# One core: a small matrix product written with the matrix as stationary operand and two vectors as moving operand, without transposes

## The chip, the cores and the metric

The kernel runs on one core of a Trainium2 chip. The metric is the device time of one execution in microseconds (us). Times inside the program are counted from the start of the profiled span.

## What is computed

The reference is one layer of a diffusion backbone: an FFN, a mixer of a convolution branch and a recurrent branch, and a second FFN, on 512 latent tokens and 256 context tokens with 1024 channels. Every normalised input is multiplied by a scale and moved by a shift, which are linear in a conditioning vector: `c` for the latent tokens, `c_ctx` for the context. Cut to what matters here:

```python
m  = jnp.split((jax.nn.silu(c)     @ lp["w_mod"] + lp["b_mod"])[:, None, :],    N_MOD, axis=-1)
mc = jnp.split((jax.nn.silu(c_ctx) @ lp["w_mod"] + lp["b_mod"])[None, None, :], N_MOD, axis=-1)
x  = x  + 0.5 * m[2]  * swiglu(modulate(rmsnorm(x,  g_n1), m[0],  m[1]),  w_ffn1_up, w_ffn1_down)
xc = xc + 0.5 * mc[2] * swiglu(modulate(rmsnorm(xc, g_n1), mc[0], mc[1]), w_ffn1_up, w_ffn1_down)
```

`w_mod` is 1024 x 9216. The change concerns its first two of nine parts alone, the first shift (`m[0]`, `mc[0]`) and the first scale (`m[1]`, `mc[1]`), which the first FFN needs.

## The kernel before

Activations lie with channels on the 128 partitions: 1024 channels are 8 blocks k of 128. `mod_first(k)`, below called **block k**, computes shift and scale of channel block k for both vectors. It loads 1 MB of `w_mod` into two tiles named `raw` of 512 KB (the pool has four such tiles, `RB = 4`), multiplies on TensorE, and writes the columns k of the tiles `M[0]` (shift) and `M[1]` (scale). The trace shows each of these fp32 matmuls as two records (a weight load and a matmul record each, two times).

Around it the program starts up in these steps:

- x (2 MB) and xc (1 MB) are loaded, a position table is added to x (L609), squares are taken on ScalarE and summed on VectorE into `acc` (latent) and `accc` (context, both L279).
- Two matmuls with a matrix of ones (L283) sum `acc` and `accc` over the partitions. ScalarE and VectorE turn them into 1/rms, `rs` and `rsc` (L303 to L309). VectorE then writes `xr` = x times `rs` and xc times `rsc` (L617, L618), 16 instructions.
- `hook1` takes the channel blocks in turn: `scale_of` makes G (L263), ScalarE applies scale and shift to `xr` (L632), and VectorE and ScalarE form sums and differences of pairs of blocks (L356 to L359) and split each into a high and a low part (L146 on ScalarE, L147 on VectorE). These are the moving operands of the first FFN. The split parts have the names nh, nl, nhc, nlc and nbx.
- The weights of the first FFN (`up`) come through the same four `raw` tiles; their sums on VectorE are L393, L394, L397 and L398, and their split is `whi` (ScalarE) and `wlo` (VectorE). The first products run on TensorE in L425 to L427.
- From then on parts 2 to 8 of `w_mod` are computed on VectorE (L234, one load of 512 KB each) while the FFN runs.

Blocks 0 to 4 are called ahead of the sums of squares, blocks 5 to 7 inside `hook1`. The order in which each engine executes comes from a scheduler that plans the whole program; each engine and the DMA queue SP then work strictly in that order. A `raw` tile is loaded anew when its last reader is done.

Of the kernel before, what the change touches and what calls it, by code (L numbers as in the profile page):

```python
# [9 lines left out]
F32 = mybir.dt.float32  # L10
# [3 lines left out]
ALU = mybir.AluOpType  # L14

P = 128
D = 1024
KB = D // P
# [49 lines left out]
def block_kernel(ctx: ExitStack, tc: tile.TileContext, io):  # L68
# [6 lines left out]
    V, S, T, GP = nc.vector, nc.scalar, nc.tensor, nc.gpsimd  # L75
# [4 lines left out]
    def region(name, side=None):  # L80
        st = ExitStack()
        return st, st.enter_context(tc.tile_pool(name=name, bufs=1, side=side, reuse_waits="tile"))
# [24 lines left out]
    def psum_small():  # L107
        return PS["pool"].tile([P, 512], F32, name="psm", bufs=PS["singles"])
# [12 lines left out]
    def v_(name, a=0, b=None):  # L121
        o, s = VOFF[name]
        return vec[:, o + a:o + (s if b is None else b)]
# [9 lines left out]
    regA, A = region("regA", "right")  # L133
# [15 lines left out]
    def wload(src, n):  # L149
        raws = []  # L150
        for a in range(0, n, 1024):
            raw = wp.tile([P, 1024], F32, name="raw", bufs=RB)
            m = min(1024, n - a)
            last["load"] = nc.sync.dma_start(raw[:, :m], src[:, a:a + m])
            raws.append(raw)
        return raws
# [30 lines left out]
    def ps_both(ps):  # L187
# [2 lines left out]

    cs = const.tile([P, KB, 2], F32, name="cs")
    S.activation(cs.rearrange("p k j -> p (k j)"), v_("c"), AF.Silu)
    c32 = A.tile([P, KB, P], F32, name="c32", tag="cb1")
    V.memset(c32, 0.0)
    V.tensor_copy(c32.rearrange("p k (q r) -> p k q r", q=4)[:, :, :, 0:2],
                  cs[:, :, None, :].to_broadcast([P, KB, 4, 2]))

    def mod_first(k):
        ps = psum_small()
        raw = wload(io["wmod01"][k], 2048)  # L200
        last["mod"] = last["load"]
        for i in range(KB):
            T.matmul(ps[:, :256], c32[:, i, :], raw[i // 4][:, (i % 4) * 256:(i % 4 + 1) * 256],  # L203
                     start=(i == 0), stop=(i == KB - 1))
        tt = A.tile([P, 256], F32, name="tt", bufs=2)
        V.transpose(tt, ps[:, :256])
        tv = tt.rearrange("p (B q r) -> p B q r", B=2, q=4)
        for q in range(4):
            r = slice(32 * q, 32 * q + 32)
            for B in range(2):  # L210
                V.tensor_tensor(M[B][r, k, :], tv[r, B, q, 0:2],
                                v_("b_mod", B * KB + k, B * KB + k + 1)[r].to_broadcast([32, 2]), op=ALU.add)

    def mod_tile(i):
        return const.tile([P, KB, 2], F32, name=f"m{i}")
# [1 line left out]
    M, G = {}, {}  # L217
# [374 lines left out]
    er = pos[:, :32].rearrange("p (b r) -> p b r", b=4)  # L592
    ec = pos[:, 32:].rearrange("p (b r) -> p b r", b=4)
    mod_first(0)
    nc.sync.dma_start(pos, io["pos"])
    nc.sync.dma_start(x[:, :4], io["x"][:, :4])
    mod_first(1)
    nc.sync.dma_start(x[:, 4:], io["x"][:, 4:])
    nc.sync.dma_start(xc, io["xc"])
    for k in range(2, 5):  # L600
        mod_first(k)
# [60 lines left out]
    e, s_, s2, q, sp, rc = (la[:, i] for i in range(6))  # L662
# [30 lines left out]
    B = regB = None  # L693
# [405 lines left out]
```

## Time and profile before

| | us |
|---|---|
| median of 3 runs (1514.05 to 1519.76) | 1518.24 |
| the profiled execution, device time | 1522.92 |
| its span in the trace | 1521.1 |
| TensorE busy | 1436.9 (94%) |
| VectorE busy | 1267.5 (83%) |
| ScalarE busy | 730.1 (48%) |

The profiled execution is 4.7 us over the median; 1.8 us of its time lie outside the span. The shares are means over the whole program. The change acts in the first 5% of it, where TensorE and VectorE are loaded quite differently from the mean.

### The profile page before, as it was taken

Reading aid. Unit: us, or ns where it says so; the run is one execution under the profiler, and the core shown is the slowest. Engines: PE = TensorE matmul, PEld = TensorE weight load, DVE = VectorE, ACT = ScalarE, POOL = GpSimd, SP = SyncE. Lnnn points to the kernel's source line nnn. Section 1 sums busy time; section 2 is a strip of 40 time slices with the busy share of each in tenths; the row PEclk is TensorE's granted clock in tenths of the full one; section 3 lists DMA queues with packets and bytes.
Section 4 is the critical chain, followed back from the end, with each engine's and each line's share of the span. In section 5 each row is a group of like instructions: output and inputs, shape, how many; then the busy total and the mean of one; then the engine's idle time right before and its main releaser. Section 6 shows DMA issues by size and latency. Waiting matters only on the chain.

```text
span 1521.1 us, 20670 instructions
## 1 busy us (share of the span) xinstructions
PE 1436.9 (94%) x8094; PEld 1285.7 (85%) x8094; DVE 1267.5 (83%) x1957; ACT 730.1 (48%) x1011; POOL 22.2 (1%) x55
## 2 busy tenths in 40 slices
PE   6699999999999999899999989999996999999997
PEld 5498898989988997688778778778896989999897
DVE  5999999785768868899999999975589958678686
ACT  3742341422313345667887863236366525435252
POOL 0000000000000000000000040000000000000000
PEclk9799999999999999899999999999997999999999
DMA  7334445361425124112222212233251333323331
GB/s 279 128 125 159 147 148 163 111 194 56 145 94 186 62 83 160 62 63 90 70 64 97 77 54 85 77 131 139 97 181 56 91 118 98 97 98 98 111 98 56
DMA packets 49346, 169.02 MB, mean 111 GB/s; under 512 B 5600, under 2 KB 7904, under 8 KB 48608
## 3 DMA queue, kind: packets, MB, share of 16 engines
q1 hardware_dynamic: 49248, 167.70, 34.2%
q8 instruction: 63, 1.03, 0.3%
q14 instruction: 35, 0.29, 0.1%
HBM read 163.48 MB, written 4.19 MB: 110 GB/s over the span
## 4 chain that ended last, share of the span: by engine, by line
PE 58%; DVE 24%; DMA 7%; issue 7%; ACT 3%; POOLq 1%; DVEq 0%; ACTq 0%; POOL 0%; SPq 0%
PE psm L173 9%; PE psm L175 9%; PE psm L177 9%; PE psm L425 8%; PE psm L427 8%; PE psm L426 8%; DVE wlo L147 5%; DMA raw<-in_wmod 4%; DVE cv L742 3%; DMA raw<-in_down 2%; PE psm L203 2%; ACT whi L146 1%; DVE raw L234 1%; POOLq L1094 1%; DVE junk L234 1%
## 5 line engine op out<-in xcount | busy, mean ns | idle before, releaser
L146 ACT ACTIVATE whi<-raw 128x1024 fp32r<-128x1024 f32 (+2 forms) x230 | 233.1, 1014 | 352.0 <-PE psm L175 232.8
L147 DVE TENSOR_TENSOR wlo<-raw,whi 128x1024 fp32r<-128x1024 f32 (+2 forms) x230 | 267.4, 1163 | 37.7 <-ACT whi L146 37.4
L742 DVE SCALAR_TENSOR_TENSOR cv<-u,vec,cv 128x512 f32<-128x512 f32 x236 | 166.6, 743 | 1.0
L173 PE MATMUL psm<-H,whi 128*128 128x256 f32 (+1 forms) x496 | 152.0, 355 | 4.5 <-ACT H L146 4.1
L175 PE MATMUL psm<-H,whi 128*128 128x256 f32 (+1 forms) x496 | 151.9, 354 | 0.0
L177 PE MATMUL psm<-H,wlo 128*128 128x256 f32 (+1 forms) x496 | 151.0, 352 | 0.0
L173 PE MATMUL psm<-nh,whi 128*128 128x512 f32 x336 | 132.3, 396 | 4.2 <-ACT u L724 2.9
L177 PE MATMUL psm<-nh,wlo 128*128 128x512 f32 x336 | 132.0, 393 | 2.2 <-DVE wlo L147 2.1
L175 PE MATMUL psm<-nl,whi 128*128 128x512 f32 x336 | 132.1, 393 | 1.7 <-DVE nl L317 1.5
L425 PE MATMUL psm<-nbx,whi 128*128 128x384 f32 x286 | 98.3, 344 | 13.2 <-ACT nbx L146 7.8
L173 PEld LDWEIGHTS psm<-H,whi 128*128 128x128 f32 x496 | 92.9, 189 | 18.9 <-ACT H L146 5.6
L175 PEld LDWEIGHTS psm<-H,whi 128*128 128x128 f32 x496 | 93.5, 189 | 13.6 <-DVE H L147 0.5
L177 PEld LDWEIGHTS psm<-H,wlo 128*128 128x128 f32 x496 | 93.7, 189 | 13.0
L426 PE MATMUL psm<-nbx,whi 128*128 128x384 f32 x286 | 97.9, 342 | 0.8 <-DVE nbx L147 0.8
L427 PE MATMUL psm<-nbx,wlo 128*128 128x384 f32 x286 | 97.3, 342 | 0.4 <-DVE wlo L147 0.3
L425 PE MATMUL psm<-nb,whi 128*128 128x256 f32 x264 | 77.3, 293 | 10.4 <-ACT nb L146 9.2
L234 DVE SCALAR_TENSOR_TENSOR raw<-raw,cb 128x1024 f32<-128x1024 f32 x56 | 68.1, 1218 | 17.4 <-DMA raw<-in_wmod 17.2
L560 DVE SCALAR_TENSOR_TENSOR x<-psm,m,x 128x512 f32<-128x512 f32 x64 | 47.7, 745 | 39.6 <-PE psm L177 39.6
L146 ACT ACTIVATE whi<-s 128x1024 fp32r<-128x1024 f32 x44 | 46.7, 1062 | 70.0 <-PE psm L426 24.6
L426 PE MATMUL psm<-nl,whi 128*128 128x256 f32 (+1 forms) x264 | 79.9, 303 | 0.0
L173 PEld LDWEIGHTS psm<-nh,whi 128*128 128x128 f32 x336 | 63.3, 189 | 18.6 <-ACT u L724 3.2
L177 PEld LDWEIGHTS psm<-nh,wlo 128*128 128x128 f32 x336 | 63.4, 189 | 17.2 <-DVE wlo L147 4.0
(296 smaller groups left out, 3794.1 us busy)
## 6 DMA issues: line engine op xcount, KB each, us to landing
raw<-in_up SPq DMA_DIRECT2D x88, 512.0 KB, 3.8
raw<-in_wmod SPq DMA_DIRECT2D x72, 512.0 KB, 4.0
raw<-in_down SPq DMA_DIRECT2D x30, 512.0 KB, 4.0
raw<-in_down SPq DMA_DIRECT2D x24, 384.0 KB, 3.2
raw<-in_wvg SPq DMA_DIRECT2D x16, 512.0 KB, 3.7
raw<-in_wout SPq DMA_DIRECT2D x16, 512.0 KB, 3.9
raw<-in_wlx SPq DMA_DIRECT2D x10, 512.0 KB, 3.7
raw<-in_wlg SPq DMA_DIRECT2D x10, 512.0 KB, 3.7
```

Source lines behind the costliest of these rows:

```text
L146: S.activation(hi, src, AF.Copy)
L147: V.tensor_tensor(lo, src, f32(hi), op=ALU.subtract)
L173: T.matmul(p_, hi[:, wk, :], h, start=first, stop=False)
L175: T.matmul(p_, hi[:, wk, :], l, start=False, stop=False)
L177: T.matmul(p_, lo[:, wk, :], h, start=False, stop=last)
L203: T.matmul(ps[:, :256], c32[:, i, :], raw[i // 4][:, (i % 4) * 256:(i % 4 + 1) * 256], start=(i == 0), stop=(i == KB - 1))
L234: V.scalar_tensor_tensor(o, raw, 1.0, cb[j], op0=ALU.mult, op1=ALU.mult, accum_out=out[:, j:j + 1])
L425: T.matmul(ps, hi[:, o + k, :], h, start=first and k == 0, stop=False, **kw)
L426: T.matmul(ps, hi[:, o + k, :], l, start=False, stop=False, **kw)
L427: T.matmul(ps, lo[:, o + k, :], h, start=False, stop=k == 3, **kw)
L560: V.scalar_tensor_tensor(x[:, d], ps[-1], g[:, d, 0:1], x[:, d], op0=ALU.mult, op1=ALU.add)
L742: V.scalar_tensor_tensor(o, u[:, t:t + SEQ], wdw[:, j, t:t + 1], o, op0=ALU.mult, op1=ALU.add)
```

## The change

A block had 8 matmuls in which the conditioning vectors were stationary: `c32`, the two columns of silu(c) put four times into 128 columns of which the others are zero. The matrix was moving, 256 columns at a time. The result lay with tokens on partitions, so VectorE turned it by a transposition in 32 x 32 squares, and eight small additions of 32 x 2 added the bias. Now a block has 16 matmuls: 128 x 128 of the matrix are stationary, two columns of `cs` are moving. The result lies with channels on partitions, and two additions of 128 x 2 are left. The tiles `c32` and `tt` are gone; so a load into the tile `cb1`, which shared its memory with `c32`, no longer waits for TensorE.

```diff
     cs = const.tile([P, KB, 2], F32, name="cs")
     S.activation(cs.rearrange("p k j -> p (k j)"), v_("c"), AF.Silu)
-    c32 = A.tile([P, KB, P], F32, name="c32", tag="cb1")
-    V.memset(c32, 0.0)
-    V.tensor_copy(c32.rearrange("p k (q r) -> p k q r", q=4)[:, :, :, 0:2],
-                  cs[:, :, None, :].to_broadcast([P, KB, 4, 2]))
 
     def mod_first(k):
         ps = psum_small()
         raw = wload(io["wmod01"][k], 2048)
         last["mod"] = last["load"]
-        for i in range(KB):
-            T.matmul(ps[:, :256], c32[:, i, :], raw[i // 4][:, (i % 4) * 256:(i % 4 + 1) * 256],
-                     start=(i == 0), stop=(i == KB - 1))
-        tt = A.tile([P, 256], F32, name="tt", bufs=2)
-        V.transpose(tt, ps[:, :256])
-        tv = tt.rearrange("p (B q r) -> p B q r", B=2, q=4)
-        for q in range(4):
-            r = slice(32 * q, 32 * q + 32)
-            for B in range(2):
-                V.tensor_tensor(M[B][r, k, :], tv[r, B, q, 0:2],
-                                v_("b_mod", B * KB + k, B * KB + k + 1)[r].to_broadcast([32, 2]), op=ALU.add)
+        for B in range(2):
+            for i in range(KB):
+                o = (i % 4) * 256 + B * P
+                T.matmul(ps[:, 2 * B:2 * B + 2], raw[i // 4][:, o:o + P], cs[:, i, :], start=(i == 0), stop=(i == KB - 1))
+        for B in range(2):
+            V.tensor_scalar(M[B][:, k, :], ps[:, 2 * B:2 * B + 2], v_("b_mod", B * KB + k, B * KB + k + 1), None, op0=ALU.add)
```

The loop over B is the outer one: the first `raw` tile of a block is read in the first four matmuls of each B, so its last reader is the 12th of the 16 matmuls. Before, it was the 4th of 8. Lines after the change have numbers that are 9 lower (L283 is now L274, L393 is L384).

The scheduler orders the start anew. Behind the first FFN block all engines have the same rows as before. On VectorE, at the place where 1/rms is made, there stood before:

```order
L211 TENSOR_TENSOR m_99<-tt,vec 32x2
L263 SCALAR_TENSOR_TENSOR G_100<-m_99,vec 128x2
L305 TENSOR_SCALAR t<-psm 128x512
L305 TENSOR_SCALAR t<-psm 128x256
L393 TENSOR_TENSOR s_481<-raw 128x512
L308 TENSOR_TENSOR t<-t 128x512
L308 TENSOR_TENSOR t<-t 128x256
L309 SCALAR_TENSOR_TENSOR rs<-t,rs 128x512
L309 SCALAR_TENSOR_TENSOR rsc<-t,rsc 128x256
L206 STREAM_TRANSPOSE tt<-psm 128x256
L617 TENSOR_TENSOR xr<-x,rs 128x512
```

and now the same place on VectorE reads:

```order
L296 TENSOR_SCALAR t<-psm 128x512
L203 TENSOR_SCALAR m_95<-psm,vec 128x2
L203 TENSOR_SCALAR m_96<-psm,vec 128x2
L296 TENSOR_SCALAR t<-psm 128x256
L254 SCALAR_TENSOR_TENSOR G_97<-m_96,vec 128x2
L299 TENSOR_TENSOR t<-t 128x512
L299 TENSOR_TENSOR t<-t 128x256
L300 SCALAR_TENSOR_TENSOR rs<-t,rs 128x512
L300 SCALAR_TENSOR_TENSOR rsc<-t,rsc 128x256
L608 TENSOR_TENSOR xr<-x,rs 128x512
```

The sum of `up` weights (L393) has left this place, and so has the transposition of block 4; the two additions of block 4 (`m`, L203) have come in ahead of the last steps of `rs`.

Further on, VectorE prepares the last operands; `raw` and `s` here are the `up` weights of the first FFN block and their sums. Before:

```order
L263 SCALAR_TENSOR_TENSOR G_100<-m_99,vec 128x2
L394 TENSOR_TENSOR s_481<-s_481,raw 128x512
L398 TENSOR_TENSOR raw<-raw 128x512
L397 TENSOR_TENSOR s_482<-s_481,raw 128x512
L357 TENSOR_TENSOR t<-xr 128x384
L358 TENSOR_TENSOR t<-xr,t 128x384
L147 TENSOR_TENSOR wlo<-s_481,whi 128x1024
```

and now, from the same `wlo` on VectorE:

```order
L348 TENSOR_TENSOR t<-xr 128x384
L147 TENSOR_TENSOR wlo<-s_478,whi 128x1024
L147 TENSOR_TENSOR nl<-xr,nl 128x768
L349 TENSOR_TENSOR t<-xr,t 128x384
L388 TENSOR_TENSOR s_479<-s_478,raw 128x512
L350 TENSOR_TENSOR t<-xr,t 128x384
L147 TENSOR_TENSOR nbx<-t,nbx 128x768
L389 TENSOR_TENSOR raw<-raw 128x512
```

The two sums that are the last readers of the first `up` tile (before L398 and L397, now L388 and L389) stood ahead of this `wlo` and now stand behind it. The additions of blocks 6 and 7 (not shown) stand together, ahead of L384.

## Rows read from the trace of the kernel before

**Rows 1.** The page: the span, and busy time, share of the span and instruction count of TensorE and VectorE.

```profile
span 1521.1 us, 20670 instructions
PE 1436.9 (94%) x8094; PEld 1285.7 (85%) x8094; DVE 1267.5 (83%) x1957; ACT 730.1 (48%) x1011; POOL 22.2 (1%) x55
```

**Rows 2.** Busy time by stretch: the stretch and its length, then busy time and instructions of PE (matmuls), PEld (weight loads), DVE (VectorE), ACT (ScalarE) and POOL, then the granted TensorE clock (1.00 is the level of 2.4 GHz, 0.50 that of 1.2 GHz), the share of the DMA engines and GB/s.

```profile
19.50:25.30 5.80, 5.71 (x13) 4.54 (x14) 5.80 (x13) 5.08 (x11) 0.16 (x2) 0.50 0.53 198
25.30:37.60 12.30, 9.09 (x40) 7.30 (x38) 7.35 (x30) 4.34 (x8) 0.00 (x0) 0.99 0.68 220
37.60:46.20 8.60, 7.40 (x24) 5.57 (x24) 8.55 (x26) 7.21 (x12) 0.00 (x0) 0.80 0.46 148
46.20:76.40 30.20, 16.64 (x55) 12.78 (x56) 29.84 (x71) 20.02 (x28) 0.00 (x0) 0.72 0.38 125
88.20:200.00 111.80, 108.05 (x601) 101.58 (x600) 105.14 (x170) 38.95 (x53) 0.00 (x0) 0.98 0.47 147
```

**Rows 3.** The chain of waits in its first stretch, in order of time: start, length, what it was (an engine's work, or a DMA from its issue to its landing).

```profile
5.84 3.77 PE psm L203 x8
...
9.62 9.93 DMA raw<-in_wmod
...
19.59 10.48 PE psm L203 x34
30.08 1.29 PE psm L283 x4
...
32.69 4.94 DMA raw<-in_wmod
...
43.12 3.69 DMA raw<-in_wmod
...
48.88 4.09 DMA raw<-in_wmod
```

**Rows 4.** The matmul records of L203 in two short stretches, 19.5 to 24.5 us and 37.6 to 39.0 us: count, and shortest, median and longest duration in ns.

```profile
L203 PE MATMUL psm<-raw,c x12: 634/634/795, 19.6 to 24.4; 128*128 128x256 f32 x12
...
L203 PE MATMUL psm<-raw,c x6: 379/379/483, 37.7 to 38.9; 128*128 128x256 f32 x6
```

**Rows 5.** The timeline up to the first multiplications by `rs`: start, length of the merged instructions together, engine, line, operation, tiles and forms, count, and in brackets the idle time before it and what ended that.

```profile
1.02 0.91 DVE L194 MEMSET c<- 128x1024 f32 x1 [1.02 <-PEq L1091]
...
25.52 0.41 DVE L279 TENSOR_TENSOR accc<-accc,t 128x256 f32<-128x256 f32 x1
...
26.71 0.93 DVE L211 TENSOR_TENSOR m<-tt,vec 32x2 f32<-32x2 f32 x8
...
31.03 0.69 ACT L303 ACTIVATE rs<-psm,epst 128x512 f32<-128x512 f32 x1 [5.03 <-PE psm L283]
31.14 0.16 DVE L263 SCALAR_TENSOR_TENSOR G<-m,vec 128x2 f32<-128x2 f32 x1
31.20 3.18 PE L203 MATMUL psm<-raw,c 128*128 128x256 f32 x14
...
33.32 0.41 ACT L307 ACTIVATE t<-rsc 128x256 f32<-128x256 f32 x1
...
34.92 0.69 DVE L393 TENSOR_TENSOR s<-raw 128x512 f32<-128x512 f32 x1 [2.15 <-DMA raw<-in_up]
35.53 1.02 DVE L308 TENSOR_TENSOR t<-t 128x512 f32<-128x512 f32 x2
...
37.40 0.44 DVE L206 STREAM_TRANSPOSE tt<-psm 128x256 f32<-128x256 f32 x1
...
37.77 0.65 DVE L617 TENSOR_TENSOR xr<-x,rs 128x512 f32<-128x512 f32 x1
38.34 0.92 DVE L211 TENSOR_TENSOR m<-tt,vec 32x2 f32<-32x2 f32 x8
...
39.27 0.42 DVE L618 TENSOR_TENSOR xr<-xc,rsc 128x256 f32<-128x256 f32 x1
```

**Rows 6.** The same timeline for the operands of the first FFN block, with the same columns; the row of SPq is the issue of DMAs.

```profile
58.60 0.15 DVE L263 SCALAR_TENSOR_TENSOR G<-m,vec 128x2 f32<-128x2 f32 x1
58.67 0.55 DVE L356 TENSOR_TENSOR t<-xr 128x384 f32<-128x384 f32 x1
59.14 0.77 DVE L206 STREAM_TRANSPOSE tt<-psm 128x256 f32<-128x256 f32 x2
59.96 0.56 DVE L147 TENSOR_TENSOR nbx<-xr,nbx 128x384 fp32r<-128x384 f32 x1
...
68.19 0.69 DVE L398 TENSOR_TENSOR raw<-raw 128x512 f32<-128x512 f32 x1
68.79 0.68 DVE L397 TENSOR_TENSOR s<-s,raw 128x512 f32<-128x512 f32 x1
...
69.55 5.82 SPq L154 DMA_DIRECT2D raw<-in_wmod  x2
...
70.45 1.22 DVE L147 TENSOR_TENSOR wlo<-s,whi 128x1024 fp32r<-128x1024 f32 x1
71.59 0.95 DVE L147 TENSOR_TENSOR nl<-xr,nl 128x768 fp32r<-128x768 f32 x1
...
78.48 1.22 DVE L234 SCALAR_TENSOR_TENSOR junk<-raw,cb 128x1024 bf16<-128x1024 f32 x1
```

## The prediction

> **What bounds the kernel now.** I read the busy times first [rows 1]: TensorE is busy for 94% of the span, so a change there looks dear and one on VectorE cheap. By stretches it is otherwise [rows 2]. From 37.6 to 76.4 us VectorE is busy 38.4 of 38.8 us, and TensorE works only now and then; from 88 us on both are nearly full (108 and 105 of 112 us). The chain of waits [rows 3] gives the order of the start: until 31 us it runs over the loads of the matrix and the matmuls of blocks 0 to 4, then over loads for blocks 5 to 7. The timeline [rows 5, 6] shows VectorE's queue: `xr` begins at 37.77, the first `wlo` of a weight sum ends at 71.6, and TensorE's dense work waits for it. Behind the first FFN block the rows of all engines are unchanged, and there is no spare room in which a delay could vanish. So I price the change by how much earlier or later that `wlo` and the first `junk` (78.48) come, and let the difference stand to the end.
>
> **VectorE: less work.** A block loses a transposition (0.37 us from 37.40 to 37.77) and eight additions (0.93) [rows 5]. It gains two additions of 128 x 2. Nearest are a small addition (0.93/8 = 0.12) and G on 128 x 2 (0.16); I take 0.12 each. The memset (0.91) lay ahead of the first matrix load, so its loss is worth nothing while that load is out until 5.8.
>
> From the start of `xr` to the end of `wlo` lie 71.59 - 37.77 = 33.8 us. Out of it go the additions of blocks 4 to 7 (4 x 0.93) and the transpositions of 5 to 7 (0.37, and 0.82 for two [rows 6]): 4.9. In come six additions, 0.7. By the new order L397 and L398 (0.60 each from start to start) and one L358 (0.47, as L356) move out and one L393 (0.60) in: -1.1. That leaves 28.5 us: 5.3 saved, if nothing waits.
>
> **TensorE: twice the records.** Before, a block was 16 records of 256 columns, spaced (3.18 - 0.379)/13 = 0.216 us at the level of 2.4 GHz [rows 4, 5] and (3.77 - 0.795)/7 = 0.425 at 1.2 GHz [rows 3, 4]. Now it is 32 records of two columns, each with a weight load of its own. No row shows one. What a load costs that nothing hides is seen at the first record after a pause, which is longer than the later ones: 795 - 634 = 161 ns at the low level, 483 - 379 = 104 ns at the high one [rows 4]. With a two-column matmul there is no work to hide it behind, so I take the load plus the columns (2/256 of 0.425) and a little for uneven spacing: **0.17 us at the low level, 0.11 at the high one**. A block is then 5.4 or 3.5 us, against 6.8 or 3.45 before. Below, TensorE could cost nothing that shows; above, each record could wait for the whole one ahead: 0.161 + (0.634 - 0.425) = 0.37 us low, 0.104 + (0.379 - 0.216) = 0.27 high.
>
> The Trainium skill (TensorE: Matmul & The Clock Gate, LDWEIGHTS) prices a load by its columns over 1.2 GHz whatever the clock, an estimate of 107 ns for 128. At the high level the trace agrees (104); at the low one it shows 161, and the measurement decides. By the page a block would cost 3.4 us at either level and the time would be near that of the first rival below.
>
> **The clock.** At 19.6, after a pause, matmuls began at the low level (0.50), and after 5.7 us of gapless 256-column streaming the high level was granted [rows 2]. Two-column records leave the array nearly without columns. No row shows whether that raises the clock; every rise in the trace came behind wide streams, and in 37.6 to 46.2, where they were broken by waits for loads, the mean was 0.80. I take it that it does not rise before the first FFN.
>
> **Walk through the new start at the low level.**
> - Blocks 0 and 1: 5.84 + 64 x 0.17 = 16.7. The raw for block 2 lands at 9.62 + 9.93 = 19.55 behind x and xc, so this is hidden.
> - Blocks 2, 3 and the first matmul of 4: 19.6 + 66 x 0.17 = 30.8 (before 30.1). The four records of L283 (two of 512, two of 256 columns) take 2.55 instead of 1.29: 33.4. The other 30 records of block 4 end at 38.5, and 0.2 later their result can be read (0.634 - 0.425).
> - VectorE now adds block 4 ahead of the last steps of `rs`: 38.7 + 0.24, then 0.42 and 0.16 for L296 and G, then 37.40 - 35.53 = 1.87 for the four steps. `xr` begins at 41.4, **3.6 later**, although the wait of 2.15 for `up` weights [rows 5] is gone: it hid nothing but is replaced by a longer one.
> - The `up` weights keep two of the four `raw` tiles, so blocks 5 to 7 share two. The first of the two is now free after 24 of 32 records, not after half. Block 5's first load: 33.4 + 22 x 0.17 = 37.1, landing 4.3 later (between 3.69 and 4.94 [rows 3]) at 41.4. From block to block 24 x 0.17 + 3.9 (mean of 3.69 and 4.09) = 8.0: block 7 starts at 57.4, its second half lands 1.4 later, and 24 records bring it to 62.9, readable at 63.1.
> - VectorE comes to block 7's additions, ahead of which 58.60 - 37.77 - 0.93 - 0.37 - 0.93 + 0.47 + 0.47 + 0.48 = 20.0 us of work lie, at 61.4. It waits 1.7 us, and all operands behind it in the queue wait with it. `wlo` ends at 41.4 + 28.5 + 1.7 = **71.6, as before**.
> - The first `up` tile is freed by L389, now behind `wlo` (six steps, 0.87 + 0.47 + 0.60 + 0.47 + 0.87 + 0.60 = 3.9): 75.5. The load behind it was issued at 69.55 [rows 6]; now it lands at 75.5 + 4.3 = 79.8, and `junk`, at 78.48 before, waits until then: **+1.4**.
>
> `cb1` loads without waiting for TensorE, but ScalarE's use of it stands in the queue ahead of block 5, whose operands come later still: nothing.
>
> **Sum:** 3.6 - 5.3 + 1.7 + 1.4 = +1.4 us. On the profiled execution that is 1522.92 + 1.4 = 1524.3; on the median, 4.7 lower, 1519.6: **1520 us**. The path from 19.6 to block 7 holds 66 + 22 + 24 + 24 + 8 + 24 = 168 of the new records, so each 10 ns in the price of one weighs 1.7 us, and a landing that is 0.5 us off weighs up to 2. The case by itself reaches from 1516 to 1526.
>
> **Rivals.**
> - *The clock rises all the same* behind the gapless two-column stream, at 25.3 as before. The first FFN's start waits for less: 33 records at 0.17, 33 at 0.11: 28.9; L283 30.2; block 4 readable at 33.7, `xr` at 36.4, block 7 (0.14 a record, as the clock may fall in between) at 56.2, ahead of VectorE's 56.4. `wlo` ends at 64.9, 6.7 earlier; the load behind L389 takes 1.3 back. -5.4: **1513**. For it speaks that engine queues stay full; against it that the columns are few. The same page (What's actually happening) ties the clock to how busy the engine was recently and does not count matmuls, so by it a stream of small ones could do.
> - *Loads overlap, TensorE hardly shows.* Then L283 follows the last sum (25.9 instead of 30.1, -4.2); ScalarE's steps, which ended at 33.7 but were read at 35.5, give -1.9, the transposition -0.4, VectorE's work -5.3, the load behind L389 +1.3: -10, **1508**. Against it: a load at the head of a stream delays its matmul by 104 to 161 ns, and nothing lies between.
> - *Each matmul waits for the one ahead*, which adds to the same two columns of PSUM: 0.37 a record. Blocks 2 and 3 then end at 53, `xr` begins at 70.4, block 7 is read at 106.5, and `wlo` ends some 43 us late: **1561**; at the high level (0.27) some 19 late, 1537. For it: the old records to one place were never closer than 0.216. Against it: they were spaced by their columns, at either level. The forecast turns into a slowdown over 0.5% (7.6 us) from (7.6 - 1.4)/168 = 0.037 more, that is from **0.21 us a record** at the low level.
>
> **How the numbers follow.** A difference under 0.5% can't be told from none in this kernel (its three runs span 0.4%). Chances: forecast 0.58 (of which 0.04 beyond +0.5%), clock rises 0.18 (0.02 beyond -0.5%), overlap 0.08, serial 0.13, and 0.03 that some other late load costs over 0.5%. Faster 0.02 + 0.08 = 0.10, slower 0.04 + 0.13 + 0.03 = 0.20, within 0.70. The range runs from 1509, which holds the risen clock and half of the overlap case, to 1530, which holds the forecast with a record of up to 0.22 us; the serial case is left out.
>
> **What would show it.** The spacing of the two-column records (0.17 or 0.11), the granted clock from 6 to 60 us, the start of `xr` (41.4), whether VectorE idles for the matmuls of block 7 near 61, the end of the first `wlo` (71.6), and a wait of `junk` for its load. A record price outside 0.15 to 0.2 or a high clock makes the prediction wrong.

## The result and the profile after

The changed kernel takes 1530.17 us (median of 4 runs, 1528.15 to 1532.17) against 1518.28 on the same chip: a ratio of 1.0077, with a 95% interval of 1.0062 to 1.0092. It is slower by 9 to 14 us. I had predicted 1520 with a range up to 1530, so the time lies at the range's upper edge, 0.2 above it, and the likeliest case (no difference) did not come. A slowdown of over 0.5% had a chance of 0.20, of which 0.04 lay with the forecast's own case. The profiled execution took 1532.17 us against 1522.92 before, 9.3 more.

The page of the changed kernel answers to [rows 1]: 17 us more of busy TensorE, 9 less of VectorE.

```profile
span 1530.4 us, 20863 instructions
PE 1453.8 (95%) x8222; PEld 1310.0 (86%) x8222; DVE 1258.4 (82%) x1899; ACT 729.9 (48%) x1011; POOL 3.8 (0%) x55
```

The stretches of [rows 2], after the change, with the same columns:

```profile
19.50:25.30 5.80, 5.80 (x29) 5.80 (x29) 5.58 (x13) 2.30 (x6) 0.00 (x0) 1.00 0.51 167
25.30:37.60 12.30, 12.30 (x53) 11.09 (x53) 4.81 (x15) 5.20 (x10) 0.00 (x0) 1.00 0.53 171
37.60:46.20 8.60, 5.29 (x36) 5.21 (x37) 6.01 (x16) 4.75 (x9) 0.00 (x0) 0.68 0.38 123
46.20:76.40 30.20, 21.75 (x93) 20.57 (x93) 20.41 (x44) 16.67 (x25) 0.00 (x0) 0.50 0.44 139
88.20:200.00 111.80, 106.87 (x598) 99.82 (x597) 105.07 (x169) 38.82 (x54) 0.00 (x0) 1.00 0.45 148
```

VectorE, full from 46.2 to 76.4 us before, is now busy for 20.4 of 30.2 us there. TensorE is full up to 37.6 us. Its granted clock reads 1.00 there, but up to 37.2 us its records have the length of the low level, as the next rows show.

The records of L201 (two columns each) in three stretches: 8 to 18 us, the same as one row of the timeline, 37.2 to 39.8 us, and 47 to 60 us; durations in ns are shortest/median/longest, and the timeline row has the start, the length and the count.

```profile
L201 PE MATMUL psm<-cs,raw x48: 352/352/352, 7.8 to 17.8; 128*128 128x2 f32 x48
...
7.77 10.38 PE L201 MATMUL psm<-cs,raw 128*128 128x2 f32 x48
...
L201 PE MATMUL psm<-cs,raw x25: 251/251/352, 37.0 to 39.8; 128*128 128x2 f32 x25
...
L201 PE MATMUL psm<-cs,raw x47: 353/353/374, 46.7 to 59.8; 128*128 128x2 f32 x47
```

A record is spaced (10.38 - 0.352)/47 = **0.213 us** from the next, for 28 us on end. From 46.2 us on, where the granted clock is 0.50, records are as long (353 ns) as in the first 18 us (352), so those were at the low level too, whatever the clock's column says. Only for some 3 us behind the wide matmuls of L274 are they shorter (251).

The chain of waits in its first stretch, with the columns of [rows 3]:

```profile
5.86 27.86 PE psm L201 x130
33.72 2.77 PE psm L274 x4
36.49 2.78 PE psm L201 x22
39.29 4.13 DMA raw<-in_wmod
43.46 7.00 PE psm L201 x32
50.48 4.83 DMA raw<-in_wmod
55.35 5.29 PE psm L201 x24
60.66 0.33 SPq L154
61.04 7.51 DMA cb<-in_cc
68.57 1.06 ACT cb L219
69.63 0.74 ACT nhc L146
```

Before, loads and matmuls took turns in the chain from the first block on. Now 130 records on end carry it up to 33.7 us: the load for block 2 has left it.

The timeline, with the columns of [rows 5, 6]:

```profile
40.19 0.35 DVE L203 TENSOR_SCALAR m<-psm,vec 128x2 f32<-128x2 f32 x2 [3.05 <-PE psm L201]
42.73 0.69 DVE L608 TENSOR_TENSOR xr<-x,rs 128x512 f32<-128x512 f32 x1
62.78 1.86 PE L201 MATMUL psm<-cs,raw 128*128 128x2 f32 x8 [2.15 <-DMA raw<-in_wmod]
67.00 5.28 PE L201 MATMUL psm<-cs,raw 128*128 128x2 f32 x24
68.57 1.06 ACT L219 ACTIVATE cb<-cb 128x1024 f32<-128x1024 f32 x1 [10.40 <-DMA cb<-in_cc]
70.39 0.96 DVE L147 TENSOR_TENSOR nhc<-t,nhc 128x768 fp32r<-128x768 f32 x1 [9.59 <-ACT nhc L146]
79.77 1.22 DVE L147 TENSOR_TENSOR wlo<-s,whi 128x1024 fp32r<-128x1024 f32 x1
80.90 0.95 DVE L147 TENSOR_TENSOR nl<-xr,nl 128x768 fp32r<-128x768 f32 x1
88.45 1.22 DVE L225 SCALAR_TENSOR_TENSOR junk<-raw,cb 128x1024 bf16<-128x1024 f32 x1
```

`xr` begins 5.0 us later than in [rows 5]; VectorE idles once for 9.6 us; the first `wlo` of a weight sum ends 80.90 - 71.59 = 9.3 us later than in [rows 6], as much as the two profiled executions differ by. Two things end late side by side: block 7's last 24 records (67.00 + 24 x 0.213 = 72.1), and the load of `cb0`, whose issue stands on SP's queue behind block 7's second load. The load lands at 68.55; ScalarE waits 10.4 us for it, and the splits that VectorE reads are queued behind that. VectorE is through with them at 72.1.

### The profile page after: what moved, and what is told of

Same layout as the page of the kernel before. It is cut to its first block, busy times and chain, and to the rows that moved or that the text cites. A ratio compares the mean times of both kernels' runs of the same rounds, so it can differ in the third digit from the quotient of the medians.

```text
span 1530.4 us, 20863 instructions
## 1 busy us (share of the span) xinstructions
PE 1453.8 (95%) x8222; PEld 1310.0 (86%) x8222; DVE 1258.4 (82%) x1899; ACT 729.9 (48%) x1011; POOL 3.8 (0%) x55
## 4 chain that ended last, share of the span: by engine, by line
PE 64%; DVE 24%; DMA 6%; ACT 3%; issue 3%; DVEq 0%; SPq 0%; ACTq 0%
PE psm L173 10%; PE psm L175 10%; PE psm L177 10%; PE psm L416 9%; PE psm L417 9%; PE psm L418 9%; DVE wlo L147 5%; DVE cv L733 4%; DMA raw<-in_wmod 3%; PE psm L201 3%; DMA raw<-in_down 2%; ACT whi L146 2%; PE ps L177 1%; DVE raw L225 1%; PE ps L173 1%
## 5 line engine op out<-in xcount | busy, mean ns | idle before, releaser
L175 PEld LDWEIGHTS psm<-nl,whi 128*128 128x128 f32 x336 | 63.5, 189 | 16.5 <-DVE nl L308 2.9
```

The costliest lines, as they stand in the source:

```text
L175: T.matmul(p_, hi[:, wk, :], l, start=False, stop=False)
```

## The experiments

The theory was that the pace of the new records sets the time; the first rival was that the load of `cb0`, which I had priced at nothing, does. The scheduler plans each edited kernel anew: `a_cb` keeps VectorE's order and `a_i` all but some rows of it, the others have an order of their own in the start, and their times include it.

**`a_cb`: both `cb` loads early.**

```
     for k in range(2, 5):
         mod_first(k)
+    cb.append(A.tile([P, D], F32, name="cb1", tag="cb1"))
+    for j in range(2):
+        with tc.issue_after(last["mod"].ins):
+            nc.sync.dma_start(cb[j], io["cc"][j:j + 1].to_broadcast([P, D]))
...
     def load_cb():
-        cb.append(A.tile([P, D], F32, name="cb1", tag="cb1"))
         for j in range(2):
-            with tc.issue_after(last["mod"].ins):
-                nc.sync.dma_start(cb[j], io["cc"][j:j + 1].to_broadcast([P, D]))
...
```

> The changed kernel with one thing moved: the two loads of cb0 and cb1 are issued right behind the load of block 4, not behind that of block 7. In the changed kernel ScalarE waited 10.4 us for cb0 and VectorE 9.6 us behind it. Theory A (the pace of the two-column records sets the end of the start; the wait for cb0 lies beside block 7, whose records end at 72 us): block 7 comes only some 2 us earlier, because its load no longer shares the DMA engines with cb0 and cb1; 1528 us. Theory B (the late load of cb0 is the loss): the 9.6 us go, 1520 us.

1529.71 us, a ratio to the kernel before of 1.0073 (1.0056 to 1.0090), so no gain that can be told. Its timeline: ScalarE's wait is gone, and VectorE waits for block 7's matmuls instead.

```profile
55.37 1.04 ACT L216 ACTIVATE cb<-cb 128x1024 f32<-128x1024 f32 x1
68.94 5.11 PE L201 MATMUL psm<-cs,raw 128*128 128x2 f32 x24
74.09 0.22 DVE L203 TENSOR_SCALAR m<-psm,vec 128x2 f32<-128x2 f32 x1 [8.55 <-PE psm L201]
```

The wait that the trace names in the changed kernel (9.6 us, by way of `cb0`) covers a second one of nearly the same end. Taking the named one away frees nothing that shows. The test is not quite clean: in this execution the 30 records of block 4 behind the wide matmuls took 6.40 us and not 3.87, since they stayed at the low level, and block 7's last 24 begin 1.9 us later than in the changed kernel (68.94 for 67.00). A gain of that size may be hidden by it.

**`a_i`: the raw tiles released earlier, at the same pace.**

```
-        ps = psum_small()
+        ps = [psum_small() for _ in range(2)]
...
-        for B in range(2):
-            for i in range(KB):
+        for i in range(KB):
+            for B in range(2):
                 o = (i % 4) * 256 + B * P
-                T.matmul(ps[:, 2 * B:2 * B + 2], raw[i // 4][:, o:o + P], cs[:, i, :], start=(i == 0), stop=(i == KB - 1))
+                T.matmul(ps[B][:, :2], raw[i // 4][:, o:o + P], cs[:, i, :], start=(i == 0), stop=(i == KB - 1))
...
```

> The changed kernel with the loop over the eight column blocks of the matrix outside and the loop over the two halves inside (each half sums into a PSUM tile of its own). Same 32 records a block, same pace; but the first raw tile of a block is free after 16 records instead of 24, so the load behind it starts 8 records earlier. Theory A (the lost time is the pace of the records plus the loads that wait for them, one after the other): blocks 5, 6 and 7 each come 8 x 0.213 = 1.7 us earlier, block 7 about 5.1 us in all, and the load of cb0 behind it too; the first wlo ends near 74.7 instead of 79.8 and the time is about 1525 us. Rival B (the loads' release does not matter, only the number of records counts): the first wlo stays at 79.8 and the time at 1530.

1526.49 us, 1.0047 (1.0029 to 1.0064): 3.7 us better than the changed kernel where theory A said 5. Its timeline shows what kept the rest:

```profile
61.66 3.41 PE L201 MATMUL psm<-cs,raw 128*128 128x2 f32 x16
63.19 1.06 ACT L219 ACTIVATE cb<-cb 128x1024 f32<-128x1024 f32 x1 [9.80 <-DMA cb<-in_cc]
65.01 0.96 DVE L147 TENSOR_TENSOR nl<-t,nl 128x768 fp32r<-128x768 f32 x1 [7.45 <-ACT nl L146]
77.31 1.22 DVE L147 TENSOR_TENSOR wlo<-s,whi 128x1024 fp32r<-128x1024 f32 x1
```

Block 7 now ends at 65.1 instead of 72.1, and `cb0`, which comes 5.4 us earlier, is the last to be waited for. The `wlo` begins 2.5 us earlier. So the loads behind the released tiles are part of the path. By this trace `cb0` does count once block 7 is out of the way; with two columns no run took both away.

**`a_n128`: 128 moving columns instead of 2.** The vector pair is read 64 times over; only two columns of the result are used.

```
-                T.matmul(ps[:, 2 * B:2 * B + 2], raw[i // 4][:, o:o + P], cs[:, i, :],
+                T.matmul(ps[:, 128 * B:128 * B + 128].rearrange("p (r j) -> p r j", j=2), raw[i // 4][:, o:o + P],
+                         cs[:, i, None, :].to_broadcast([P, 64, 2]),
...
```

> The changed kernel with a wider moving operand: the two columns of cs are read 64 times over, 128 columns a matmul, of which two are used. Nothing else is changed. Theory A1 (a record costs its weight load, 256 cycles, whatever the columns up to 128; and TensorE's clock stays low because two columns leave the array nearly idle): spacing stays 0.21 us at the low level, the high level is granted near 25 us, then 0.107 a record; the start ends some 10 us earlier, 1518 us with the wait for cb0 left. Theory A2 (the columns do not matter to the clock): spacing 0.21 us up to 60 us, 1530 us as the changed kernel. Theory C (columns add to the load): 0.21 + 0.11 us a record, slower, 1540 us.

1521.15 us, 1.0009 (0.9998 to 1.0020): 64 times the columns, and 9 us faster than the changed kernel, where theory A1 said 12. The timeline from 7 to 10 us, the records of 6.5 to 10 and of 12 to 15 us, and three stretches by the columns of [rows 2]:

```profile
6.74 3.62 PE L201 MATMUL psm<-cs,raw 128*128 128x128 f32 x16
...
L201 PE MATMUL psm<-cs,raw x17: 421/421/553, 6.4 to 9.9; 128*128 128x128 f32 x17
...
L201 PE MATMUL psm<-cs,raw x28: 273/273/377, 11.7 to 15.0; 128*128 128x128 f32 x28
...
19.50:25.30 5.80, 5.56 (x33) 5.37 (x34) 5.66 (x12) 5.71 (x12) 0.00 (x0) 0.71 0.41 166
25.30:37.60 12.30, 9.13 (x74) 8.41 (x73) 7.00 (x21) 5.75 (x11) 0.00 (x0) 1.00 0.78 247
37.60:46.20 8.60, 6.23 (x30) 5.64 (x28) 8.60 (x18) 5.20 (x9) 0.00 (x0) 0.60 0.27 85
```

At first the spacing is (3.62 - 0.421)/15 = 0.213 us, the same as with two columns: up to 128, the moving columns don't set it. Then the records shorten from 421 to 273 ns, and again within 19.5 to 25.3, where the granted clock is 0.71 and 1.00 from there on. In each of the four kernels with 128 columns the records shorten between 9 and 12 us; in the changed kernel, `a_cb` and `a_i`, all with two columns, none does before 36.9. In the code the width is all that differs between this kernel and the changed one; VectorE's order differs too, but TensorE's gapless first block does not hang on that. From 37.6 to 46.2 us, where the blocks wait for loads, the clock is back at 0.60.

**`a_warm`: two-column records that begin at the high level.** Eight matmuls of 128 x 512 on constants run ahead of block 0.

```
+    wide = A.tile([P, 512], F32, name="wide")
+    GP.memset(wide, 1.0)
+    pw = psum_small()
+    for i in range(8):
+        T.matmul(pw, ones, wide, start=(i == 0), stop=(i == 7))
...
```

> The changed kernel with eight matmuls of 128 x 512 on constants ahead of block 0 (their sum is used by nothing), so that the two-column stream begins at the high clock. It delays block 0, so its time is not the point. Theory A (a stream of two-column matmuls does not keep the clock high, and a record takes 256 cycles at either level): the spacing is 0.107 us at first and goes back to 0.213 within the stream, without a pause. Rival B (the stream is enough to keep a clock that is already high; it was only too little to raise it): 0.107 until the pause for block 2's load at least. Rival C (the pace does not depend on the clock): 0.213 from the first record on.

Stretches, the records of 10.3 to 15 and of 16 to 22 us, and the timeline from 10.4 to 12.6:

```profile
10.20:15.20 5.00, 5.00 (x47) 4.96 (x45) 2.04 (x6) 0.95 (x2) 0.00 (x0) 1.00 1.03 428
15.20:20.20 5.00, 5.00 (x27) 5.00 (x26) 2.39 (x8) 2.38 (x6) 0.00 (x0) 0.51 0.96 373
...
L208 PE MATMUL psm<-cs,raw x44: 168/251/252, 10.2 to 15.0; 128*128 128x2 f32 x44
...
L208 PE MATMUL psm<-cs,raw x30: 352/352/353, 15.7 to 21.9; 128*128 128x2 f32 x30
...
10.38 2.37 PE L208 MATMUL psm<-cs,raw 128*128 128x2 f32 x20
```

As theory A had it. At the high level a record is spaced (2.37 - 0.251)/19 = 0.112 us; the stream goes on without a pause, and at about 15.2 us the granted clock falls to 0.50 and the records to 352 ns. These also are the lengths of the changed kernel's start, now with the clock's column beside them. A stream of two-column matmuls neither raised the clock nor kept it high. The time of this single run (1533.78 us) holds the delay of block 0 and says nothing more.

**`b_nodve`: VectorE's half of the change alone.** The kernel before, with its wide matmuls, but with the two additions of the change in place of the transposition and the eight additions; it reads the sums untransposed, so the first shift and scale are not those of the reference.

```
-        V.transpose(tt, ps[:, :256])
...
+        for B in range(2):
+            V.tensor_scalar(M[B][:, k, :], ps[:, 2 * B:2 * B + 2], v_("b_mod", B * KB + k, B * KB + k + 1), None, op0=ALU.add)
```

> The kernel before, with its eight wide matmuls a block, but VectorE's transpositions and small additions left out; two additions of 128 x 2 stand in their place and read the untransposed sums, so shift and scale hold wrong numbers, and the time is that of the saved work alone. Theory: VectorE is the limit from 37 to 76 us, so its 5.3 us come back, 1513 us. Rival: the loads and matmuls of blocks 5 to 7 or the load of cb1 set the end of the start, and nothing comes back: 1518 us.

1513.50 us, 0.9970 (0.9957 to 0.9984): 2.4 to 6.5 us are to be had from VectorE, in line with the 5.3 of the working, and the changed kernel is 16.7 us slower than this, which is what TensorE's half costs together with the order that the scheduler made for it. The profiled execution is the slowest of its eight (1517.94), and in it the gain is not seen at the `wlo`: VectorE waits again, for block 7.

```profile
57.17 0.22 DVE L206 TENSOR_SCALAR m<-psm,vec 128x2 f32<-128x2 f32 x1 [4.23 <-PE psm L203]
70.66 1.22 DVE L147 TENSOR_TENSOR wlo<-s,whi 128x1024 fp32r<-128x1024 f32 x1
```

In this kernel's own order the `wlo` is not the place to read the gain. From 109.6 us on VectorE's rows are again those of the kernel before, and there it is 2.7 us ahead (106.91 for 109.58); the two profiled executions differ by 5.0. That there is a gain rests on the times.

**`a_n128_cb`: 128 columns and early `cb` loads.**

> Both edits: 128 moving columns and the early loads of cb0 and cb1. Theory A1: TensorE's blocks as quick as before the change, VectorE's 5.3 us saved, no wait for cb0: 1513 us, below the kernel before. Theory A2: as the early loads alone, 1528 us. Theory B (cb0 is the loss): no different from the early loads alone, 1520 us.

1518.82 us, 0.9998 (0.9986 to 1.0011), 5.8 us short of the 1513 that was expected. At the faster pace the early `cb` loads are worth some 2 us (1521.15 - 1518.82), about what two such medians can tell apart. But block 5's first load, issued behind them at 32.52, now takes 5.9 us to land (4.0 in `a_n128`, 33.03 to 37.06), and its records, (6.38 - 0.421)/31 = 0.19 us apart, are for the most part back at the low level:

```profile
38.45 6.38 PE L201 MATMUL psm<-cs,raw 128*128 128x128 f32 x32 [5.06 <-DMA raw<-in_wmod]
55.17 0.22 DVE L203 TENSOR_SCALAR m<-psm,vec 128x2 f32<-128x2 f32 x1 [3.78 <-PE psm L201]
65.57 0.22 DVE L203 TENSOR_SCALAR m<-psm,vec 128x2 f32<-128x2 f32 x1 [4.90 <-PE psm L201]
```

I had forgotten that a load put ahead of others is a delay for them: from 32 to 34 us the share of the DMA engines is 1.00 here and 0.46 in `a_n128`. VectorE waits for block 7 (4.90) and the one ahead of it (3.78).

**`a_n128_i` and `a_n128_cb_i`: 128 columns with the early release**, the second with the early `cb` loads too (the edits above together).

> The same loop order with each vector pair read 64 times over (128 moving columns, of which two are used). Theory A: the columns raise the clock from about 10.6 us on as in the run with 128 columns (1521.2), and the earlier release takes 8 records off each of blocks 5 to 7, at 0.11 to 0.21 us a record 2.6 to 5.1 us in all: 1516 to 1518.5, below the kernel before by 0 to 2.5 us. Rival B (the order of the records holds nothing): 1521.

> The same as the run before it, and the loads of cb0 and cb1 issued right behind the load of block 4. In the run with 128 columns and early cb loads (1518.8) VectorE still waited 3.8 and 4.9 us for the matmuls of blocks 6 and 7. Theory A: the earlier release of the raw tiles takes 2.6 to 5.1 us out of these waits, 1514 to 1516. Rival B: the loads of cb stand ahead of block 5's on the queue and set its start, so only blocks 6 and 7 gain (1.8 to 3.4 us), 1515.4 to 1517. Rival C: no gain, 1518.8.

1516.21 us (0.9981, 0.9970 to 0.9992) and **1514.85 us (0.9967, 0.9955 to 0.9979)**, 12 runs each. The second beats both kernels, by 3.2 to 6.8 us against the kernel before. Its timeline and the stretch up to the `wlo`:

```profile
35.16 0.68 DVE L609 TENSOR_TENSOR xr<-x,rs 128x512 f32<-128x512 f32 x1
...
48.47 2.02 PE L201 MATMUL psm<-cs,raw 128*128 128x128 f32 x16 [0.62 <-DVE t L347]
52.00 2.05 PE L201 MATMUL psm<-cs,raw 128*128 128x128 f32 x16 [1.32 <-DMA raw<-in_wmod]
65.28 1.23 DVE L147 TENSOR_TENSOR wlo<-s,whi 128x1024 fp32r<-128x1024 f32 x1
...
46.20:65.30 19.10, 11.90 (x67) 9.94 (x67) 19.05 (x40) 14.38 (x22) 0.00 (x0) 0.83 0.32 108
```

Block 7 is done by 54, VectorE is busy for 19.05 of 19.1 us up to the `wlo`, and that begins 70.45 - 65.28 = 5.2 us earlier than in [rows 6]: VectorE has nothing left to wait for there. That this is near the 5.3 us that the prediction worked out for VectorE's work is luck: 37.77 - 35.16 = 2.6 of it is the earlier start of `xr`, and the other 2.6 is work up to a `wlo` that stands at another place of this kernel's order.

## Why the prediction came out as it did

- **The price of a record: the step that failed.** I took 0.17 us at the low level from how much longer the first record after a pause is (161 ns). It measured 0.213 at the low and 0.112 at the high level, outside the 0.15 to 0.2 that the prediction gave as its own test. A nearer price was in the rows, in another place: 256 columns were spaced 0.425 us at the low and 0.216 at the high level [rows 3, 4, 5], so 128 columns at those rates take 0.2125 and 0.108. That loading 128 columns takes as long as streaming 128 is the likely reading; no run varied the stationary columns, so another floor of the same size is not excluded. The 161 ns were not the price of a record. By the prediction's own count, 168 records x 0.043 = 7.2 us come on top, and 1.4 + 7.2 = 8.6 is near the 9.3 measured; it had named 0.21 us as the point from which it turns into a slowdown. That nearness is in part luck. Block 7 ends 9.2 late: 7.2 for the price, 3.7 for loads that took more than I had summed (28.6 us from the start of block 5 to the end of block 7 for 21.5, less 3.4 for 80 records), and 1.7 back for 17 records of block 4 at the high level.
- **The Trainium skill's price of a load** (TensorE: Matmul & The Clock Gate, LDWEIGHTS), by estimate 107 ns for 128 columns, has no term for the clock: the 0.112 of the high level are near it, the 0.213 of the low one are twice that. The measurement decides.
- **The clock stays low before the first FFN: right**, but for some 3 us behind L274. That the same page of the Trainium skill (What's actually happening) ties the clock to how busy the engine was did not help to tell: by the trace TensorE was busy without a pause and yet the clock stayed low, and in `a_warm` it fell.
- **The walk through the start: right in its order, late by the price.** Block 1 is added at 19.7 (16.7), L274 begins at 33.6 (30.8), block 4 is added at 40.2 (38.7) and `xr` begins at 42.7 (41.4). The burst at the high level gave back part.
- **Blocks 5 to 7: 9 us too early.** I had its last records end at 62.9; they end at 72.1. Of that, 2.1 is the late start of block 5 (43.46 for 41.4); two rounds of 24 records and a load were 9.7 us instead of 8.0, 3.3; the second half of block 7's matrix came 4.2 us behind the first instead of 1.4 (67.00 - 62.78), 2.8; and the last 24 records took 1.0 more. I had let the first raw tile set the round; the chain goes over the second, which is free only after all 32 records.
- **VectorE waits for block 7, 1.7: a wait there is, of another size.** In the changed kernel it idles 9.6 us for a split that is queued behind `cb0`, and comes to block 7's additions just as they can be made, at 72.2. With `cb0` early it idles 8.6 us for block 7 itself (`a_cb`).
- **"ScalarE's use of it ... nothing": right in the end, wrong in the reason.** I looked at `cb1` and did not walk SP's queue for `cb0`. The wait is 10.4 us and is named in the chain, but it lies beside block 7's (`a_cb`). At a faster pace it costs perhaps 1.4 to 2.3 us (the medians of the two pairs of runs with 128 columns).
- **VectorE's work from `xr` to the end of `wlo`, 28.5: right.** 80.90 - 42.73 = 38.2 less the idle 9.6 and 0.2 of smaller gaps is 28.4.
- **`junk` waits 1.4 for its load: wrong.** (By its own numbers, 79.8 - 78.48, this should have read 1.3.) `junk` is 10.0 late, 0.7 more than `wlo`, and waits for nothing: its load was issued when L389 was done, at 84.94, but landed 3.2 us later and not 4.3, while VectorE had other work until 88.45.
- **The rivals.** Each matmul waiting for the one ahead (0.37) falls: the spacing, 0.213, is shorter than a record, 0.352. So does the hidden load. The risen clock did not come by itself; where wide operands brought it, the time was 1521 and not 1513: blocks 5 to 7, which wait for loads, ran mostly at the low level again (0.60 from 37.6 to 46.2 us), and VectorE idled 7.8 us for block 7.
- **Nothing came back later: so in these two executions, which is in part luck.** The difference of 9.3 at the `wlo` is that of their times. But VectorE's rows are those of the kernel before only from 93.88 us on, where the changed kernel is 10.0 behind (103.89); the medians differ by 11.9; and `a_cb`'s profiled execution, 10.9 us behind at that row (104.77), ends only 1527.43 - 1522.92 = 4.5 behind it. A single execution carries a few us of its own behind the start.

## What to carry to other kernels

Price a float32 record of TensorE by the larger of its moving and its stationary columns, both at the rate that wide records show, at the clock level of that stretch (seen here with 128 stationary and 2, 128 and 256 moving columns); swapping the operands so that a narrow one moves makes the loads the work. When the chain of waits names one late thing, look for what ends within a microsecond or two beside it before you move it, and take both away together. The place of one instruction compares two kernels only as far as the order up to it is the same. Walk every load on the queue behind one that you delay, and count from the release of the last tile that a block holds.

## What the runs showed of the hardware

- A float32 record with a load of 128 x 128 of its own was spaced 0.213 us at the low level and 0.112 at the high one; at the low level it was the same with 2 and with 128 moving columns.
- A stream of two-column records without a pause stayed at the low level for 28 us, and let a clock that was high fall (`a_warm`). With 128 columns, at first at the same spacing, the records shortened to those of the high level within the first block. Reading the same two columns 64 times over cost no spacing at the low level, and the time fell by 9 us.
- The granted clock of the profile read 1.00 in the start of the changed kernel, up to 37.2 us, where the lengths of the records (352 ns, the same as at 0.50) showed the low level. Read the lengths of one shape beside the clock's column.
